# Attention's product with v turned round and scaled behind it, and an earlier bound for the seven-product form, in a two-layer trunk

## Chip, cores and metric

The kernel runs on one core of one Trainium2 chip. The metric is the device time of one execution in microseconds (us); the kernel before is given by the median of three runs.

## What is computed

One sequence of 1024 tokens of width 1024 passes two layers. Layer 0 mixes by sliding-window attention (8 query heads of 64, 2 key heads, window 128) and a gated delta rule (4 heads of 128); layer 1 by a recurrent block (RG-LRU). Each layer ends in a squared-relu MLP of width 4096, and a layer norm stands behind each mixer and each MLP. All of it is float32. The part that the change touches, cut from the reference:

```python
def sliding_window_attention(q, k, v, sinks):      # in blocks of W = 128 queries
    kb, vb = band(k), band(v)                      # the block before and this block
    s = jnp.einsum('bnqhgd,bnkhd->bnhgqk', qb, kb) * (DH ** -0.5)
    s = jnp.where(mask, s, -jnp.inf)
    p = jax.nn.softmax(jnp.concatenate([s, sink], axis=-1), axis=-1)[..., :-1]
    o = jnp.einsum('bnhgqk,bnkhd->bnqhgd', p, vb)

def sqrelu_mlp(x, w1, w2):
    h = jax.nn.relu(x @ w1)
    return (h * h) @ w2
...
for layer in range(DEPTH):                         # DEPTH = 2
    x = layer_norm(DN_ALPHA * x + mix, ...)
    x = layer_norm(DN_ALPHA * x + sqrelu_mlp(x, ...), ...)
```

## The kernel before

The 1024 tokens are two halves, c = 0 and c = 1, of 512 tokens (four blocks of 128). A large product goes in three passes of the faster type fp32r: each float32 operand is split into a high and a low part (a cast and a subtraction on ScalarE and VectorE), and `mm3` issues high x high, high x low, low x high into one PSUM bank. Such a pass over 128x512 is one record in the trace. A product of plain float32 operands is two records.

The order of TensorE's instructions is fixed when the kernel is built. A planner (`Clock`) keeps an estimated time for every engine; generators for the two halves (`stream`), and side streams (`mixers`: attention blocks, the middle part of the delta rule, layer norms), hand out their next matmul when the planner thinks its operands ready. TensorE, VectorE, ScalarE and SP (which issues most of the loads) run in the order written.

All calls on the other engines go through one helper, L178 in the profile; matmuls through L206, transposes by TensorE through L210. So rows are told apart by the names of tiles: `mm` and `mx` are PSUM banks, `ws` a loaded weight block, `wh`/`wl` its parts, `g` large tiles, `t`, `s`, `f` smaller ones, `vraw` the values of a block, `asc` the small numbers of an attention block, `csb` the constants with the identity matrix, `parked` tiles that wait in DRAM, `t_0_0_105` and its kind sums of weights in DRAM.

`attn_block` handles one block of 128 queries and all 8 heads. It multiplies queries and keys, masks, takes the exponentials (one ScalarE call for each head, with their sum), scales each head's probabilities by the reciprocal of that sum (again a ScalarE call each), transposes them on TensorE, copies the transposed tiles out of PSUM, and multiplies: v's 64 columns are the weights, 512 columns of probabilities move. The sum over the two key blocks gathers in one bank. The block gives 4 such products (2 in the very first block).

The second half's heads: `head_front` makes k, q and v of a delta-rule head by projection and convolution, `head_z` its gate z. For later heads the projections are made early and parked in DRAM (`park`: product, copy, store by SP) and loaded again (`f<-parked`). `head_mid` inverts a triangular matrix in four levels (`t<-t` matmuls of 32x32, between VectorE operations on `t`) and then runs the scan. When a half's mixer is done, `mix_out` loads the residual (`g<-x`, four loads of 512 KB on ScalarE's queue), makes the output projection (`out_proj`) and the layer norm.

`mlp` takes the hidden dimension in eight blocks (e = 0 to 7). `straight` does one block by plain products; `seven` does two by seven products in place of eight, with sums of weight quarters that `w2_sums` makes in DRAM (for each sum a 1 MB copy by SP, then a 1 MB load with accumulation by POOL; the two are issued 8 us or more apart by the planner's clock in layer 0). A half turns from `straight` to `seven` at an even block when there is room: half 1 at once, half 0 only when the other half has finished its projection (`sts[1]["op"]`). `first(j)` makes the eight hidden blocks that the first `seven` needs.

Of the kernel before, what the change touches and what calls it, by code (L numbers as in the profile page):

```python
# [12 lines left out]
AF = mybir.ActivationFunctionType  # L13
ALU = mybir.AluOpType
# [3 lines left out]
P = 128  # L18
# [6 lines left out]
GB = 14  # L25
# [188 lines left out]
def trunk(ctx: ExitStack, tc, I, out):  # L214
    nc = tc.nc
    clk = Clock(tc, nc)
    V, G, S, PE = clk.engine(nc.vector, "V"), clk.engine(nc.gpsimd, "G"), clk.engine(nc.scalar, "S"), clk
    DS, DA, DG = clk.engine(nc.sync, "V"), clk.engine(nc.scalar, "V"), clk.engine(nc.gpsimd, "V")
    at = lambda *a: lambda: clk.ready(*a)
# [12 lines left out]
    def nm(s):  # L232
        uid[0] += 1
        return f"{s}_{uid[0]}"

    rings = dict(RINGS, g=GB)
# [39 lines left out]
    def mx_ps():  # L276
        return clk.tile("mx", 4, pmx.tile([P, 512], F32, tag="mx", name=nm("mx")))

    def v4(a):
        return a.rearrange("p (a b) -> p a b", a=4)  # L280

    def bc_last(a, n):
        return a.unsqueeze(2).to_broadcast([P, a.shape[1], n])
# [9 lines left out]
    ident, U, M1 = C["ident"], C["U"], C["M1"]  # L293
# [100 lines left out]
    def split_ps(h, l, ps):  # L394
        S.copy(h, ps)
        V.tensor_tensor(l, ps, h, ALU.subtract)
# [134 lines left out]
    def mlp(layer, c, yT, yg, ls, res, tail=False):  # L531
# [185 lines left out]

        hids = {}
        e = 0
        while e < 8 and not ((c == 1 or sts[1].get("op", -1) >= layer) and rings["g"] >= 2 and e % 2 == 0):  # L720
            if e == 7:
                res["start"]()
            yield from straight(e, e == 7)
            e += 1
# [93 lines left out]
    def attn_block(c, n, st, oT, tl, o):  # L818
        vr = st["v"][n]
        yield from wait(lambda: "ok" in o)  # L820
        qT, kT = o["qT"], o["kT"]
        pk, pv = att["kT"], att["v"]
        keys = ([(pk, pv)] if pk is not None else []) + [(kT, vr)]
        att["kT"], att["v"] = kT, vr
        k0 = 2 - len(keys)
        w = len(keys) * P
        sc = cpool.tile([P, 40], F32, tag="asc", name=nm("asc"), bufs=2)
        mx, nmx, den, es = (sc[:, i * 8:(i + 1) * 8] for i in range(4))
        pm = []
        for gp in range(2):  # L830
            yield lambda: max(clk.ready(qT, kT), clk.bank("mx", 4, 2))
            ps = [mx_ps().rearrange("p (g k) -> p g k", g=2) for _ in range(2)]
            for g2 in range(2):
                g = 2 * gp + g2
                for i, (kk, _) in enumerate(keys):
                    for h in range(2):
                        PE.matmul(ps[h][:, g2, i * P:(i + 1) * P], qT[h * 64:(h + 1) * 64, g * P:(g + 1) * P],
                                  kk[h * 64:(h + 1) * 64, :], start=True, stop=True)
            for h in range(2):
                pt = tl[2 + 2 * gp + h].rearrange("p (g k) -> p g k", g=2)  # L840
                for g2 in range(2):
                    i = 2 * (2 * gp + g2) + h
                    V.tensor_tensor_reduce(pt[:, g2, :w], ps[h][:, g2, :w], C["amask"][:, k0 * P:], 1.0, NEG,
                                           ALU.add, ALU.max, mx[:, i:i + 1])
                pm.append(pt)
        V.scalar_tensor_tensor(nmx, mx, -0.125, nsink, ALU.mult, ALU.min)
        V.tensor_tensor(es, W["sinks"], nmx, ALU.add)
        for m in range(4):
            for g2 in range(2):
                i = 2 * (2 * (m // 2) + g2) + m % 2  # L850
                S.activation(pm[m][:, g2, :w], pm[m][:, g2, :w], AF.Exp, bias=nmx[:, i:i + 1], scale=0.125,
                             accum_out=den[:, i:i + 1])
        S.activation(es, es, AF.Exp)
        V.tensor_tensor(den, den, es, ALU.add)
        V.reciprocal(den, den)
        for m in (0, 2, 1, 3):
            for g2 in range(2):
                i = 2 * (2 * (m // 2) + g2) + m % 2
                S.activation(pm[m][:, g2, :w], pm[m][:, g2, :w], AF.Copy, scale=den[:, i:i + 1])
        yield at(*pm)  # L860
        po = mx_ps()
        pend = None
        for i, (_, vv) in enumerate(keys):
            for h in range(2):
                ps = mx_ps()
                for g in range(4):
                    PE.transpose(ps[:, g * P:(g + 1) * P], pm[2 * (g // 2) + h][:, g % 2, i * P:(i + 1) * P], ident)
                pT = tl[(6, 7, 2, 3)[2 * i + h]]
                (S.copy if h else V.tensor_copy)(pT, ps)
                yield at(pT)  # L870
                PE.matmul(po[h * 64:(h + 1) * 64, :], vv[:, h * 64:(h + 1) * 64], pT, start=(i == 0),
                          stop=(i == len(keys) - 1))
        h, l = oT.quad(0, n)
        split_ps(h, l, v4(po))
        yield lambda: 0.0


# [497 lines left out]
    sts = st  # L1375
# [32 lines left out]
    while streams or mixers:  # L1408
        m = next((m for m in mixers if m[0]() + MARGIN <= clk.now), None) if clk.bank("mx", 4) <= clk.now else None
# [144 lines left out]
```

## Time and profile before

| | |
|---|---|
| median of 3 runs | 2275.01 us (2270.06 to 2276.08) |
| profiled execution, its own time | 2275.25 us |
| its span | 2273.5 us |
| TensorE busy | 2212.7 us, 97% of the span |
| VectorE busy | 1546.0 us, 68% |
| ScalarE busy | 1048.4 us, 46% |
| chain that ended last | TensorE 85%, VectorE 7%, ScalarE 5%, DMA 2% |

A row of the timeline gives a start, a duration, the engine, the line, the operation, output<-inputs, the sizes and a count; a time in square brackets is idle time ahead of it, with the engine and tile that ended it. The records of pipelined matmuls overlap in a timeline (0.4 us for one, while the next starts 0.23 us later), so the cost of a matmul is read from the distance of two starts.

### The profile page before, as it was taken

The page shows a single profiled execution, that of the slowest core. Times are in us where ns is not written, and L with a number is a line of the kernel's source. Part 1 is how long each engine was busy: PE and PEld are TensorE (multiplying, and loading weights), DVE is VectorE, ACT ScalarE, POOL GpSimd, SP SyncE. Part 2 cuts the span into 40 slices and gives each one's busy share as a digit, 9 for nine tenths or more (in the row PEclk, how much of TensorE's full clock was granted, in tenths as well). Part 3 has the DMA queues.
Part 4 walks back from the last instruction along what each step waited for, and adds up shares of the span by engine and source line. Part 5 has one row for each costly group of instructions (what it writes and reads, how often), then busy time and mean ns, then how long its engine had stood idle before and what let it go on. Part 6 is the DMA issues. An engine that isn't in the chain of part 4 may idle for free.

```text
span 2273.5 us, 31954 instructions
## 1 busy us (share of the span) xinstructions
PE 2212.7 (97%) x12436; PEld 1788.5 (79%) x12436; DVE 1546.0 (68%) x2809; ACT 1048.4 (46%) x1878; POOL 28.6 (1%) x56
## 2 busy tenths in 40 slices
PE   8999999989999999999999999999999999999997
PEld 7776877758778887888887878878788887888886
DVE  6787676576555567596567898685566657776477
ACT  5365456244322344454444677373434444444442
POOL 0000000000000000000000000000000000000000
PEclk9999999989999999999999999999999999999999
DMA  4121223256667766677765333323533443444341
GB/s 162 57 77 49 94 79 112 84 181 181 188 199 221 210 209 201 205 251 224 237 214 184 126 134 115 127 83 98 179 103 123 140 145 128 150 169 146 122 164 67
DMA packets 89945, 337.46 MB, mean 148 GB/s; under 512 B 9921, under 2 KB 10305, under 8 KB 81601
## 3 DMA queue, kind: packets, MB, share of 16 engines
q1 hardware_dynamic: 76688, 280.56, 36.2%
q0 software_dynamic: 4608, 33.56, 7.8%
q10 hardware_dynamic: 8496, 21.30, 2.7%
q8 instruction: 97, 1.59, 0.3%
q14 instruction: 56, 0.45, 0.1%
HBM read 324.37 MB, written 78.12 MB: 177 GB/s over the span
## 4 chain that ended last, share of the span: by engine, by line
PE 85%; DVE 7%; ACT 5%; DMA 2%; issue 1%; ACTq 0%; SPq 0%; DVEq 0%
PE mm L206 67%; PE mx L206 17%; DVE g L178 2%; PE mx L210 2%; DVE wl L178 2%; ACT g L178 1%; DVE s L178 1%; ACT s L178 1%; ACT wh L178 1%; DVE t L178 1%; DVE f L178 1%; ACT t L178 1%; ACT f L178 1%; DMA f<-parked 1%; DMA parked<-r 0%
## 5 line engine op out<-in xcount | busy, mean ns | idle before, releaser
L206 PE MATMUL mm<-g,wh 128*128 128x512 f32 x2816 | 885.6, 396 | 1.1 <-DVE g L178 1.1
L178 DVE TENSOR_TENSOR wl<-ws,wh 128x1024 fp32r<-128x1024 f32 (+1 forms) x444 | 538.3, 1212 | 398.9 <-ACT wh L178 394.4
L178 ACT CAST wh<-ws 128x1024 fp32r<-128x1024 f32 (+1 forms) x356 | 371.3, 1043 | 663.4 <-PE mm L206 551.3
L206 PEld LDWEIGHTS mm<-g,wh 128*128 128x128 f32 x2816 | 521.5, 189 | 109.1 <-DVE g L178 2.8
L206 PE MATMUL mm<-g,wl 128*128 128x512 f32 x1408 | 550.3, 391 | 0.0
L206 PE MATMUL mm<-wh,s 128*128 128x512 f32 x1152 | 377.4, 394 | 0.7 <-DVE g L178 0.7
L206 PEld LDWEIGHTS mm<-g,wl 128*128 128x128 f32 x1408 | 265.4, 188 | 56.5
L206 PEld LDWEIGHTS mm<-wh,s 128*128 128x128 f32 x1152 | 216.9, 188 | 46.5 <-ACT s L178 1.1
L206 PE MATMUL mm<-wh,g 128*128 128x512 f32 (+1 forms) x768 | 240.0, 384 | 7.1 <-ACT wh L178 6.8
L206 PE MATMUL mm<-wl,s 128*128 128x512 f32 x576 | 224.8, 390 | 0.0
L206 PE MATMUL mx<-wh,s 128*128 128x512 f32 x576 | 187.9, 392 | 1.5 <-DVE s L178 1.5
L206 PEld LDWEIGHTS mm<-wh,g 128*128 128x128 f32 x768 | 143.3, 191 | 34.1 <-ACT wh L178 6.8
L178 ACT CAST s<-g 128x512 fp32r<-128x512 f32 x172 | 104.7, 622 | 103.2 <-PE mm L206 54.2
L178 DVE TENSOR_TENSOR s<-g,s 128x512 fp32r<-128x512 f32 x172 | 116.0, 685 | 44.3 <-ACT s L178 44.2
L206 PE MATMUL mm<-wl,g 128*128 128x512 f32 (+1 forms) x384 | 144.2, 375 | 0.2 <-DVE wl L178 0.2
L206 PEld LDWEIGHTS mx<-wh,s 128*128 128x128 f32 x576 | 108.2, 188 | 24.6 <-DVE s L178 2.4
L206 PEld LDWEIGHTS mm<-wl,s 128*128 128x128 f32 x576 | 108.6, 189 | 21.4 <-issue 0.2
L206 PE MATMUL mx<-wl,s 128*128 128x512 f32 x288 | 112.1, 389 | 0.0
L178 DVE CAST wh<-ws 128x1024 fp32r<-128x1024 f32 x88 | 60.4, 687 | 65.0 <-PE mm L206 57.7
L178 DVE TENSOR_TENSOR g<-g,mm 128x512 f32<-128x512 f32 x136 | 89.0, 682 | 11.9 <-PE mm L206 11.3
L178 ACT ACTIVATE g<-mm 128x512 f32<-128x512 f32 x100 | 59.2, 592 | 75.2 <-PE mm L206 75.2
L206 PEld LDWEIGHTS mm<-wl,g 128*128 128x128 f32 x384 | 73.5, 192 | 11.6 <-DVE wl L178 0.5
(234 smaller groups left out, 2390.7 us busy)
## 6 DMA issues: line engine op xcount, KB each, us to landing
ws<-w SPq DMA_DIRECT2D x232, 512.0 KB, 3.4
ws<-t SPq DMA_DIRECT2D x96, 512.0 KB, 3.4
t<-w POOLq DMA_DIRECT2D x32, 1024.0 KB, 9.1
ws<-hin_fm SPq DMA_DIRECT2D x32, 512.0 KB, 3.3
t<-w SPq DMA_DIRECT2D x16, 1024.0 KB, 6.8
t<-t SPq DMA_DIRECT2D x16, 1024.0 KB, 6.3
ws<-rin SPq DMA_DIRECT2D x32, 512.0 KB, 3.3
ws<-hout SPq DMA_DIRECT2D x16, 512.0 KB, 3.7
```

Source lines behind the costliest of these rows:

```text
L178: r = f(*a, **k)
L206: ins = self.pe.matmul(out, lhsT, rhs, start=start, stop=stop, skip_group_check=fresh)
L210: return self._pe(self.pe.transpose(out, x, ident), out, [x], 0.00042 * 2 * out.shape[-1])
```

## The change

Two places are edited. In `attn_block` the product is turned: the transposed probabilities of one head (128x128) are the weights and v's 64 columns move, 16 products a block (8 in the first). The probabilities are no longer scaled on ScalarE before it; the result, in which queries lie on partitions, is scaled by one VectorE operation with the broadcast reciprocals, and four transposes bring it back to the layout that the next step needs. The copies of the transposed probabilities are shared between ScalarE and VectorE by another rule. In `mlp`, half 0 of layer 0 may turn to `seven` when the second half has finished three heads' scans and four large tiles are free; half 0 with the other half's projection done, and half 1, go as before. In every other case it now asks for `GB` = 14 free large tiles, which is all there are.

```diff
@@ -717,7 +717,9 @@
 
         hids = {}
         e = 0
-        while e < 8 and not ((c == 1 or sts[1].get("op", -1) >= layer) and rings["g"] >= 2 and e % 2 == 0):
+        room = lambda: rings["g"] >= (2 if c == 1 or sts[1].get("op", -1) >= layer else
+                                      4 if layer == 0 and sts[1].get("scan", 0) >= 3 else GB)
+        while e < 8 and not (room() and e % 2 == 0):
             if e == 7:
                 res["start"]()
             yield from straight(e, e == 7)
@@ -853,25 +855,33 @@
         S.activation(es, es, AF.Exp)
         V.tensor_tensor(den, den, es, ALU.add)
         V.reciprocal(den, den)
-        for m in (0, 2, 1, 3):
-            for g2 in range(2):
-                i = 2 * (2 * (m // 2) + g2) + m % 2
-                S.activation(pm[m][:, g2, :w], pm[m][:, g2, :w], AF.Copy, scale=den[:, i:i + 1])
-        yield at(*pm)
-        po = mx_ps()
-        pend = None
-        for i, (_, vv) in enumerate(keys):
-            for h in range(2):
+        pT = {}
+        for h in range(2):
+            yield at(pm[h], pm[2 + h])
+            for i in range(len(keys)):
                 ps = mx_ps()
                 for g in range(4):
                     PE.transpose(ps[:, g * P:(g + 1) * P], pm[2 * (g // 2) + h][:, g % 2, i * P:(i + 1) * P], ident)
-                pT = tl[(6, 7, 2, 3)[2 * i + h]]
-                (S.copy if h else V.tensor_copy)(pT, ps)
-                yield at(pT)
-                PE.matmul(po[h * 64:(h + 1) * 64, :], vv[:, h * 64:(h + 1) * 64], pT, start=(i == 0),
-                          stop=(i == len(keys) - 1))
+                pT[i, h] = tl[(6, 7, 2, 4)[2 * h + i]]
+                (S.copy if i else V.tensor_copy)(pT[i, h], ps)
+                yield lambda: 0.0
+        yield at(*pT.values())
+        po = mx_ps()
+        for g in range(4):
+            for h in range(2):
+                o = po[:, (2 * g + h) * 64:(2 * g + h + 1) * 64]
+                for i, (_, vv) in enumerate(keys):
+                    PE.matmul(o, pT[i, h][:, g * P:(g + 1) * P], vv[:, h * 64:(h + 1) * 64], start=(i == 0),
+                              stop=(i == len(keys) - 1))
+        y = tl[3]
+        V.tensor_tensor(y.rearrange("p (i d) -> p i d", i=8), po.rearrange("p (i d) -> p i d", i=8), bc_last(den, 64),
+                        ALU.mult)
+        yield at(y)
+        ps = mx_ps()
+        for g in range(4):
+            PE.transpose(ps[:, g * P:(g + 1) * P], y[:, g * P:(g + 1) * P], ident)
         h, l = oT.quad(0, n)
-        split_ps(h, l, v4(po))
+        split_ps(h, l, v4(ps))
         yield lambda: 0.0
 
 
```

The order of instructions changes from the attention blocks on. On TensorE, a part of one attention block before (`mx_3795` is the bank that gathers the result, `g_146` and `g_147` hold probabilities, `t` is a delta-rule head at its level steps, `mm` a projection):

```order
L206 MATMUL mx_3795<-g_147,vraw_325 64x512
L210 MATMUL mx_3828<-csb,g_146 128x128 x2
L210 MATMUL mx_3828<-csb,g_147 128x128 x2
L206 MATMUL mm_3770<-g_2008,wh_3766 128x512
L206 MATMUL mm_3770<-g_2009,wh_3766 128x512
L206 MATMUL mm_3770<-g_2008,wl_3767 128x512
L206 MATMUL mx_3837<-t_3388 32x32 x16
L206 MATMUL mm_3770<-g_2008,wh_3766 128x512
L206 MATMUL mm_3770<-g_2009,wh_3766 128x512
L206 MATMUL mm_3770<-g_2008,wl_3767 128x512
L206 MATMUL mx_3795<-g_147,vraw_325 64x512
```

and after, the end of the products of a block (`t_1733` belongs to a delta-rule head):

```order
L206 MATMUL mx_2074<-vraw_315,g_146 128x64
L206 MATMUL mx_2074<-vraw_320,g_147 128x64
L206 MATMUL mx_2074<-vraw_315,g_147 128x64
L206 MATMUL mx_2074<-vraw_320,g_147 128x64
L206 MATMUL mx_2074<-vraw_315,g_146 128x64
L206 MATMUL mx_2074<-vraw_320,g_147 128x64
L210 MATMUL mx_2092<-csb,t_1733 128x128 x4
L206 MATMUL mm_1994<-g_234,wh_1990 128x512
L206 MATMUL mm_1994<-g_236,wh_1990 128x512
L206 MATMUL mm_1994<-g_234,wl_1991 128x512
```

The products of a block now stand in one piece behind all its transposes; the four transposes back (from `g_146`) follow a good twenty rows later, behind products of two projections.

At the end of the second half's heads, VectorE works in this order before (`t_4413` is the head at its level steps; `f_5070` and `f_5071` belong to a gate, the `f_56` tiles to convolutions of the last head, `wh` and `wl` to weights):

```order
L178 SCALAR_TENSOR_TENSOR f_5070<-f_5070,f_5071 128x512
L178 TENSOR_TENSOR t_4413<-t_4413,mx_5195 128x128
L178 STREAM_TRANSPOSE t_4413<-t_4413 128x128
L178 TENSOR_TENSOR g_4833<-f_5070,g_4832 128x512
L178 SCALAR_TENSOR_TENSOR f_5643<-f_5642,sm,f_5643 128x512 x3
L178 TENSOR_TENSOR t_4413<-mx_5224,csb 128x128
L178 SCALAR_TENSOR_TENSOR f_5654<-f_5653,sm,f_5654 128x512 x3
L178 TENSOR_TENSOR t_4413<-t_4413,mx_5251 128x128
L178 CAST wh_5420<-ws_5418 128x1024
L178 STREAM_TRANSPOSE t_4413<-t_4413 128x128
L178 SCALAR_TENSOR_TENSOR f_5665<-f_5664,sm,f_5665 128x512
```

and after (`t_4644` is the head, `f_5104` and `f_5248` belong to gates, `f_5105` and `f_5249` are their loads):

```order
L178 TENSOR_TENSOR t_4644<-mx_5167,csb 128x128
L178 SCALAR_TENSOR_TENSOR f_5104<-f_5104,f_5105 128x512
L178 TENSOR_TENSOR s_5113<-r_5152,s_5112 128x512
L178 TENSOR_TENSOR t_4644<-t_4644,mx_5194 128x128
L178 TENSOR_TENSOR g_4802<-f_5104,g_4801 128x512
L178 STREAM_TRANSPOSE t_4644<-t_4644 128x128
L178 TENSOR_TENSOR t_4644<-mx_5223,csb 128x128
L178 TENSOR_TENSOR wl_5431<-ws_5428,wh_5430 128x1024
L178 TENSOR_TENSOR t_4644<-t_4644,mx_5268 128x128
L178 STREAM_TRANSPOSE t_4644<-t_4644 128x128
L178 TENSOR_TENSOR t_4644<-mx_5296,csb 128x128
L178 SCALAR_TENSOR_TENSOR f_5248<-f_5248,f_5249 128x512
```

The steps on `t` now alternate with the multiplications of two gates, of which each needs a tile loaded from DRAM; before, one gate and the convolutions stand there. On ScalarE, the residual loads of the second half's output projection stood among the copies of a parked tile and of the layer norm (`r_5067` is a parked tile on its way, `g_4818` to `g_4832` are normed activations and mixer outputs):

```order
L178 CAST wh_5366<-ws_5364 128x1024
L178 COPY r_5067<-mm_5024 128x512
L178 DMA g_7293<-x 128x1024 x2
L178 DMA g_7294<-x 128x1024
L178 CAST g_4832<-f_4941 128x512
L178 ACTIVATE f_5001<-f_5002 128x512
L178 DMA g_7294<-x 128x1024
L178 CAST g_4820<-mx_5096 128x4x128
```

and now stand among weights of the MLP and of the projection (`g_7369` is a hidden block of `first`):

```order
L178 CAST wh_7448<-ws_7446 128x1024
L178 CAST wh_7478<-ws_7476 128x1024
L178 ACTIVATE g_7369<-mm_7377 128x512
L178 DMA g_7404<-x 128x1024 x2
L178 DMA g_7405<-x 128x1024
L178 ACTIVATE g_7369<-g_7369 128x512
L178 DMA g_7405<-x 128x1024
L178 CAST wh_7509<-ws_7507 128x1024
L178 CAST wh_7551<-ws_7549 128x1024
```

They moved behind the norm and behind the last head's scan. SP's order there is, before:

```order
L178 DMA parked_5066<-r_5067 128x512
L178 DMA ws_5522<-w_0 128x1024
L178 DMA f_5071<-parked_5066 128x512
L178 DMA f_5642<-parked_4089 128x512
L178 DMA t_0_0_105<-w_0 128x2048
L178 DMA f_5653<-parked_4148 128x512
L178 DMA f_5664<-parked_4286 128x512
L178 DMA ws_5579<-w_0 128x1024
L178 DMA ws_5721<-w_0 128x1024
L178 DMA t_0_0_106<-w_0 128x2048
```

and after:

```order
L178 DMA f_4999<-parked_4994 128x512
L178 DMA t_0_0_105<-w_0 128x2048
L178 DMA parked_5100<-r_5101 128x512
L178 DMA ws_5487<-w_0 128x1024
L178 DMA f_5105<-parked_5100 128x512
L178 DMA ws_5551<-w_0 128x1024
L178 DMA parked_5244<-r_5245 128x512
L178 DMA ws_5595<-w_0 128x1024
L178 DMA f_5249<-parked_5244 128x512
L178 DMA t_0_0_106<-w_0 128x2048
L178 DMA parked_5324<-r_5325 128x512
```

The stores and loads of three parked gates now stand between the copies of the first two sums (`t_0_0_105`, `t_0_0_106`), where before there were the loads of one gate and of the last head. The counts: TensorE has 30 products of 64x512 (v as weights, by the order's own way of naming) fewer, 120 of 128x64 and 32 transposes of 128x128 more; all products of 128x512 on split operands are as many as before; ScalarE has 64 scalings fewer, VectorE 8 operations of 128x512 more; the number of DMAs is the same. Half 0 of layer 0 turns to `seven` at its fifth block (e = 4) in both; in the changed order the first hidden block of `first` (24 products, `mm_7377`) stands ahead of the second half's output projection, and 96 products lie between the issue of the residual loads and the first row that uses one.

## Rows read from the trace of the kernel before

**Rows 1.** The page: the span, the busy time of the engines, and the granted clock in 40 slices of the span.

```profile
span 2273.5 us, 31954 instructions
...
PE 2212.7 (97%) x12436; PEld 1788.5 (79%) x12436; DVE 1546.0 (68%) x2809; ACT 1048.4 (46%) x1878; POOL 28.6 (1%) x56
...
PEclk9999999989999999999999999999999999999999
```

**Rows 2.** Windows of the zone of the last heads of the second half. Columns: the stretch and its length; busy time and number of instructions of TensorE, its weight loads, VectorE, ScalarE and POOL; granted clock; DMA share; GB/s.

```profile
461.00:472.00 11.00, 8.68 (x74) 6.84 (x73) 11.00 (x20) 8.72 (x14) 0.00 (x0) 1.00 0.40 138
472.00:481.00 9.00, 6.49 (x69) 4.58 (x73) 8.55 (x16) 4.34 (x8) 0.00 (x0) 0.62 0.99 385
490.00:498.00 8.00, 2.91 (x42) 1.98 (x41) 3.22 (x6) 2.45 (x4) 0.00 (x0) 0.98 0.50 117
498.00:508.00 10.00, 9.77 (x69) 6.99 (x70) 4.03 (x8) 3.05 (x5) 0.10 (x1) 0.50 0.32 105
```

**Rows 3.** Waits of TensorE in 440:525: what it waited for, us in total, times, longest.

```profile
PE mx L206 <- DVE t L178: 8.2, 5, 4.7
PE mx L210 <- DVE g L178: 3.1, 1, 3.1
```

**Rows 4.** Timeline of TensorE around one old product with v (first half). Columns: start, duration, engine, line, operation, output<-inputs, rows*columns of the array, size of the moving operand, count.

```profile
118.89 0.40 PE L206 MATMUL mm<-g,wl 128*128 128x512 f32 x1
119.21 1.07 PE L206 MATMUL mx<-g,vraw 128*64 128x512 f32 x2
120.22 0.66 PE L210 MATMUL mx<-csb,g 128*128 128x128 f32 x4
```

**Rows 5.** Groups of instructions by form: the old product with v (records; busy time, mean ns).

```profile
L206 PE MATMUL mx<-g,vraw 128*64 128x512 f32 x60 | 32.2, 618 | 0.0
```

**Rows 6.** Timeline of TensorE: the distance of records. Two starts with 36 products of the split form between them (first lines); 128x16 moving columns; four transposes and eight records of 128x128; 64x64.

```profile
22.35 0.62 PE L206 MATMUL mm<-g,wh 128*128 128x512 f32 x2
...
30.52 0.39 PE L206 MATMUL mm<-g,wh 128*128 128x512 f32 x1
...
32.56 0.51 PE L206 MATMUL mx<-dsc,csb 128*128 128x16 f32 x4
32.92 0.48 PE L206 MATMUL mm<-g,wh 128*128 128x512 f32 x1
...
448.78 0.60 PE L210 MATMUL mx<-csb,t 128*128 128x128 f32 x4
449.22 1.06 PE L206 MATMUL mx<-t 128*128 128x128 f32 x8
450.11 0.28 PE L206 MATMUL mx<-t,t 128*128 128x128 f32 x1
...
516.17 0.67 PE L206 MATMUL mx<-t,t 64*64 64x64 f32 x8
516.78 0.38 PE L206 MATMUL mx<-S,t 128*128 128x128 f32 x1
```

**Rows 7.** First half: a wait of TensorE and ScalarE's work ahead of it (the first row is from the chain of waits of 180:192, start, us, what; then ScalarE's timeline, TensorE's, and the form of the scalings and exponentials).

```profile
182.46 4.05 ACT g L178 x16
...
187.22 0.61 ACT L178 ACTIVATE s<-f 128x512 f32<-128x512 f32 x1
...
188.76 0.55 PE L210 MATMUL mx<-csb,s 128*128 128x128 f32 x3 [3.23 <-DVE s L178]
...
L178 ACT ACTIVATE g<-g,asc 128x256 f32<-128x256 f32 x112 | 50.7, 496 | 9.1 <-DVE asc L178 9.1
```

**Rows 8.** The zone of the last heads: three pieces of the chain of waits of 440:500 (start, us, what); then timeline rows of ScalarE (ACTq is its DMA issue) and of POOL.

```profile
470.67 7.59 DMA parked<-r
...
478.34 3.77 DMA f<-parked
...
487.25 7.31 DMA f<-parked
...
469.11 1.05 ACT L178 CAST wh<-ws 128x1024 fp32r<-128x1024 f32 x1
469.39 0.83 ACTq L178 DMA_DIRECT2D g<-x  x2
470.05 0.59 ACT L178 COPY r<-mm 128x512 f32<-128x512 f32 x1
...
482.19 0.63 ACT L178 ACTIVATE f<-f 128x512 f32<-128x512 f32 x1 [2.20 <-DMA f<-parked]
...
486.09 0.94 POOL L178 DMA_DIRECT2D t<-w  x1 [310.58 <-DMA t<-w]
```

**Rows 9.** DMA issues of 400:560: tiles, queue, count, KB each, median us from issue to landing.

```profile
g<-x ACTq DMA_DIRECT2D x4, 512.0 KB, 7.8
...
f<-parked SPq DMA_DIRECT2D x7, 256.0 KB, 3.3
parked<-r SPq DMA_DIRECT2D x4, 256.0 KB, 2.1
```

**Rows 10.** Timeline of TensorE (two waits at level steps) and of VectorE (a gate's multiplication).

```profile
476.82 0.65 PE L206 MATMUL mx<-t 32*32 32x32 f32 x32 [1.73 <-DVE t L178]
...
498.23 0.65 PE L206 MATMUL mx<-t 32*32 32x32 f32 x32 [4.69 <-DVE t L178]
...
482.86 0.69 DVE L178 SCALAR_TENSOR_TENSOR f<-f,f 128x512 f32<-128x512 f32 x1 [2.15 <-ACT f L178]
```

## Prediction

> **What bounds the kernel now.** The page comes first: TensorE is busy for 97% of the span, and its clock stands at nine tenths or more in all fortieths of the span but one, the ninth, from 455 to 512 us [rows 1]. Its instructions run in the order in which the planner wrote them, so the time can fall only if its own work gets shorter or one of its waits goes. The profiled execution took 2275.25 us, 0.24 above the median of the three timed runs, so the sum below is made against 2275.25 and needs no correction. That slice is also where the diff moves work, the end of the second half's heads, so I split it into windows [rows 2]. Four things are to be seen. In 461:472 VectorE is busy for 11.00 of 11.00 us and TensorE for 8.68. In 472:481 the DMA share is 0.99 and the granted clock 0.62. In 490:498 TensorE works for 2.91 of 8.00 us. In 498:508 the clock is 0.50, that is, the lower of its two levels (1.2 GHz) all through, right after a stretch in which TensorE had little work. The waits of TensorE in the zone [rows 3] are 8.2 us for VectorE's `t` (level steps of a head) and 3.1 us for VectorE's `g` (the layer norm). What the two edits can give is therefore small: a per mille of the time for the product with v, and some of those waits.
>
> **The product with v.** It goes by records: each of the 30 old products is two records of 128x512, and takes 120.22 - 119.21 = 1.01 us; the record ahead of it lasts 119.21 - 118.89 = 0.32 us in place of the 0.227 of its kind [rows 4, 6], so entering the narrow form costs 0.09. The 30 cost 30 x 1.10 = 33.0 us of TensorE, all on the path, since TensorE hardly idles; there are 60 records in the trace [rows 5]. In their place stand 120 products of 128x64, two records each, so 240, and 32 more transposes. A record of 128x128 with new weights each time takes (450.11 - 449.22) / 8 = 0.111 us; one with 16 moving columns (32.92 - 32.56) / 4 = 0.090, so an eighth of the columns saves a fifth; the shortest kind, 64x64, (516.78 - 516.17) / 8 = 0.076; a transpose (449.22 - 448.78) / 4 = 0.110 [rows 6]. 64 columns lie between 16 and 128, so I take 0.100: 240 x 0.100 + 32 x 0.110 = 27.5 us. That **saves 5.5 us**. (A product of 128x512 in the split form takes (30.52 - 22.35) / 36 = 0.227, three of them to a step [rows 6]; this is used below.) The bounds are 0.111 (30.1, saves 2.9) and 0.076 (21.8, saves 11.2).
>
> **The scaling behind the product.** 64 scalings on ScalarE go, 56 of them 128x256 (half of the 112 rows of that form; the others are exponentials, which stay) [rows 7], and 8 VectorE products over 128x512 come. ScalarE is busy for less than half of the span [rows 1], so nearly all of this lies beside other work. One place doesn't: in the first half TensorE waits 3.23 us before 188.76 for the tile `s` of a head, whose tanh at 187.22 stood on ScalarE behind eight exponentials, 4.05 us from 182.46 [rows 7]. The scalings themselves come after it. But with another length of each block the planner places them elsewhere, and in the changed order no tanh of such a tile stands behind exponentials, though the start of a convolution still does. I take **2 us** off, since something else may be late there; the ends are 0 and 3.2. The new VectorE operation of 0.7 us (as others over 128x512, 0.69 [rows 10]) is waited for by four transposes of a block, but these are run as a side stream that TensorE reaches late, with other products ahead; nothing is charged for it, and at most 8 x 0.7 = 5.6 if none of it is hidden.
>
> **What the `room` edit moves.** It allows `seven` where the second half has finished three of its heads. The order shows that the switch comes at the same block (the fifth, e=4) in both kernels, so as many products of 128x512 are issued as before: the edit **does not give what its words say**, fewer products. What it does is to let the first of the eight hidden blocks of `first`, the work ahead of the first seven, go before the second half's output projection (24 products). With it the four residual loads on ScalarE's queue, 512 KB each, move: before, they are issued from 469.39 on [rows 8], and fill the DMA rows of 472:481. There the store of a parked tile takes 7.59 us where its fellows take a median of 2.1 [rows 8, 9], and SP's queue, all following loads with it, waits behind it: the next load of a parked tile starts at 478.34. In the changed order they stand beside the products of the second half's projection, with 96 products, 21.8 us, ahead of the first use; such a load takes 7.8 us [rows 9], so that is cover enough. If it weren't, the price would be the rest of one load, below 8.
>
> In the layer-norm stretch the order now has five parked projections (120 products, 27 us at 0.227) between the projection and the end of the norm, in place of four and level steps that need VectorE. Before, TensorE waits there 3.1 [rows 3] and 1.73 [rows 10], and the 0.62 of clock over 9.00 us means 6.8 us at half speed, with TensorE busy for 6.49 of 9.00: 6.8 x 0.72 / 2 = 2.4 lost. I leave 1 us of wait and no half clock: **-3.8 and -2.4**. Ends: nothing, and the whole 7.2.
>
> Behind the norm the level steps of the last head now stand between the loads of gates z1, z2 and z3, where before they stood between two gates and the convolutions. VectorE runs in order, so a gate's multiplication that waits for its load holds the level step behind it, and TensorE with it. That is the **new wait**. Before, the stretch cost 8.2 - 1.73 = 6.4 us of waits, its longest 4.69 at 498.23 [rows 10], and some 5 us by the half clock (10 us at 0.50, TensorE busy for 9.77 [rows 2]). After, by hand for z1: cast 1.05, copy 0.59, store 2.1, load 7.3 (the length of the one beside POOL's accumulation issued at 486.09; 3.3 otherwise), tanh 0.63, multiplication 0.69, and some 2.2 of smaller steps and hops (transpose, split, a step over 128x128): 14.6 [rows 8 to 10]. TensorE has 45 products and two steps meanwhile, 45 x 0.227 + 2 x 0.5 = 11.2 (a step's 32 records end within 0.65 of their start [rows 10]), so it waits 3.4. For z2 the load is the 3.3 one and a cast of 0.7 stands ahead: 11.3 against 36 products and three steps, 9.5: 1.8. For z3 the copy of the second sum is queued ahead of it, so 14.6 again, against 30 products, three steps and z2's wait, 10.0: 4.6 (0.6 with a short load). Together 9.8, which is 3.4 more than before; the half clock stays as it was. **+3.4**, from -2 (all loads 3.3) to +26 (rival 2).
>
> Sum: -5.5 - 2 - 3.8 - 2.4 + 3.4 = -10.3, and 2275.25 - 10.3 = **2265.0**. A measurement of this kernel can tell about 0.3%, 6.8 us, from no change.
>
> **A rule against it.** A record with 16 columns costs four fifths of one with 128 [rows 6], so in both what counts is loading the weights, not the columns. The Trainium skill, TensorEngine Tiling (Array Packing), section When to Use Tiling, advises for a right side of 64 columns or fewer the swap of stationary and streaming operand; before is that swapped form, and the change undoes it. What that would make of the time here is the third rival.
>
> **The rivals.** (1) *The waits only change places*: the layer norm keeps its stalls because VectorE remains full there [rows 2], and the level steps take 3.4 more. Then -5.5 - 2 + 3.4 = -4.1, **2271**. For it speaks that VectorE had no free microsecond in 461:472; against it that the level steps, the work which needs it, leave that stretch.
>
> (2) *Slower: each of the three gate loads lies beside a 1 MB copy of the sums and is waited for in full.* Each then exposes 7.4 us, and each wait brings a stretch of half clock like that of 498:508, 5 us: 3 x 12.4 = 37.2 in place of 11.4, +25.8. With the other terms, -13.7, the time is **2287**. It decides from about 25 us of loss in that stretch. For it: a load beside the accumulation took 7.31 where the median is 3.3 [rows 8, 9]. Against: the sums come every 8 us or more, one after another, and the walk above finds only two of three beside one.
>
> (3) *The turned product loads its weights in the open.* If loading (0.090) and the columns (an eighth of the 0.505 of an old record, 0.063) add up, a record takes 0.153, and 240 x 0.153 + 3.5 = 40.2, which is 12.7 more than taken: **2278**. Against it: with 128 columns the two together took 0.111 [rows 6], so they overlap.
>
> (4) *The columns decide*: 240 x 0.063 + 3.5 = 18.6, 8.9 less than taken: **2256**. Against it the 16-column row.
>
> **How the numbers follow.** Forecast 0.45, its own range 2257 to 2272 from the terms' ends. Rival 1: 0.25. Rival 2: 0.15. Rival 3: 0.07. Rival 4: 0.08. The bound for faster is 2268.2: of the forecast 0.32 lies below it, of rival 1 0.06, of rival 4 all 0.08, so 0.46. Slower needs 2282: 0.14 of rival 2 and 0.03 of rival 3, so 0.17. The rest, 0.37, is within 0.3%. The range 2254 to 2280 leaves out most of rival 2 and a little below.
>
> **What would show it.** The turned product: 16 records of 128x64 (eight of a block's 16 products) that take 16 x 0.100 = 1.6 us from the first to the next instruction, 1.8 or 1.2 at the bounds, 2.45 by rival 3. The scaling: the wait of 3.23 before 188.76 at about 1. The layer norm: no wait above 1 us there and a clock of 1.00, with the parked stores at 2 us; a stretch at 0.5 or waits of 5 in sum would be rival 1. The level steps: three waits of about 3.4, 1.8 and 4.6 for VectorE's `t`, each with a load of a parked tile behind it; above 20 us in sum is rival 2. The residual loads: no wait of the projection's accumulation for them. The forecast falls if later stretches, where the two orders agree, change by more than 2 us, since nothing above speaks of them.

## The result, and the profile after

The changed kernel takes 2276.93 us (median of 20 runs, 2270.09 to 2280.89) against 2269.74 for the kernel before in the runs beside it: **1.0029 times as long (95% interval 1.0021 to 1.0038)**, slower by some 6.6 us. The forecast was 2265, with 2254 to 2280 as its range; measured from 2275.25 it said 0.45% faster. The profiled execution took 2280.89 us, 5.6 more than the one before, so the two traces show a difference of about the size to be explained. Both traces are of long executions: 2275.25 lies 5.5 above the median of the 20 runs of before, 2280.89 lies 4.0 above that of the changed kernel.

The page after, to be held against [rows 1]:

```profile
span 2279.1 us, 32326 instructions
...
PE 2211.1 (97%) x12648; PEld 1815.2 (80%) x12648; DVE 1550.8 (68%) x2818; ACT 1022.4 (45%) x1813; POOL 28.5 (1%) x56
...
PEclk9999999989999999999999999999999999999999
```

TensorE is busy for 1.6 us less, in a span that is 5.6 us longer: it stands idle for 7.2 us more. The windows of the zone of the last heads, as in [rows 2]:

```profile
461.00:472.00 11.00, 10.74 (x107) 8.29 (x106) 8.06 (x15) 5.82 (x10) 0.94 (x1) 1.00 0.62 140
472.00:481.00 9.00, 1.68 (x22) 1.08 (x23) 2.41 (x5) 2.29 (x4) 0.00 (x0) 0.80 0.47 158
...
490.00:498.00 8.00, 7.56 (x123) 5.58 (x122) 3.74 (x7) 1.58 (x3) 0.82 (x1) 1.00 0.76 251
498.00:508.00 10.00, 2.37 (x24) 1.75 (x22) 2.26 (x5) 2.96 (x6) 0.00 (x0) 0.84 0.56 118
```

The layer norm's stretch is mended: VectorE is no longer full in 461:472 (8.06 us), and TensorE works for 10.74 of 11.00 us. But in 472:481 and 498:508 TensorE works for 1.68 and 2.37. The waits of TensorE in 440:525, for [rows 3]:

```profile
PE mx L206 <- DVE t L178: 15.6, 4, 7.6
```

The wait for VectorE's `g` is gone; that for `t`, the level steps, went from 8.2 to 15.6 us. Where it comes from is read from the chain of waits of 440:515 (start, us, what), with the issues of POOL (timeline) and VectorE's row below it:

```profile
465.00 2.35 DMA parked<-r
...
467.37 9.81 DMA f<-parked
...
490.98 3.03 DMA parked<-r
...
494.07 10.89 DMA f<-parked
...
464.91 0.94 POOL L178 DMA_DIRECT2D t<-w  x1 [286.38 <-DMA t<-w]
493.66 0.82 POOL L178 DMA_DIRECT2D t<-w  x1 [27.81 <-DMA t<-w]
...
505.71 0.69 DVE L178 SCALAR_TENSOR_TENSOR f<-f,f 128x512 f32<-128x512 f32 x1 [10.79 <-ACT f L178]
```

Two gates' loads of 256 KB take 9.81 and 10.89 us, issued 2.5 and 0.4 us behind an accumulation of 1 MB on POOL's queue; in the second case VectorE stands 10.79 us in front of the gate's multiplication, with a level step behind it, and TensorE waits. The load between the two, beside no accumulation, took 3.6.

To see where the 5.6 us went, I added up, over each stretch of both traces, by how much the distance of two starts of TensorE exceeds the usual one of that form (stalls and half clock together; the sums are worked out from all rows of a trace, and depend on what is taken as usual by some 0.4 us). The first row also has what the product itself saves, 2.6:

| stretch | forecast | traces |
|---|---|---|
| heads, to 450 us | -7.5 (product -5.5, scaling -2) | +1.6 |
| zone of the last heads, 450 to 525 | -2.8 (norm -6.2, level steps +3.4) | +0.6 |
| the rest | 0 | +3.4 |
| sum | -10.3 | +5.6 |

Of the 15.9 us between forecast and traces, 9.1 lie in the heads, 3.4 in the zone and 3.4 behind it. The zone of the last heads is, by this count, hardly worse than before; it loses its time by other waits.

### The profile page after: what moved, and what is told of

Read it like the earlier page. It is cut to its first block, busy times and chain, and to the rows that moved or that the text cites. A ratio compares the mean times of both kernels' runs of the same rounds, so it can differ in the third digit from the quotient of the medians.

```text
span 2279.1 us, 32326 instructions
## 1 busy us (share of the span) xinstructions
PE 2211.1 (97%) x12648; PEld 1815.2 (80%) x12648; DVE 1550.8 (68%) x2818; ACT 1022.4 (45%) x1813; POOL 28.5 (1%) x56
## 4 chain that ended last, share of the span: by engine, by line
PE 86%; DVE 6%; ACT 3%; DMA 2%; issue 1%; ACTq 0%; SPq 0%; DVEq 0%
PE mm L206 68%; PE mx L206 17%; DVE g L178 2%; PE mx L210 2%; DVE wl L178 1%; DMA f<-parked 1%; DVE s L178 1%; ACT s L178 1%; ACT wh L178 1%; ACT t L178 1%; DVE t L178 0%; ACT f L178 0%; DMA ws<-w 0%; ACT g L178 0%; DMA parked<-r 0%
## 5 line engine op out<-in xcount | busy, mean ns | idle before, releaser
L206 PEld LDWEIGHTS mm<-wl,g 128*128 128x128 f32 x384 | 73.5, 192 | 11.2 <-issue 0.5
```

Source lines behind the costliest of these rows:

```text
L206: ins = self.pe.matmul(out, lhsT, rhs, start=start, stop=stop, skip_group_check=fresh)
```

## The experiments

All ratios are to the kernel before on the same chip, with 95% intervals; "moved alone" below means the third run.

**Which edit, and are the sums to blame?** Four kernels; the edits are

```diff
 pv_only            # the turned product with the old condition for seven
 room_only          # the old product with the new condition
 after_sums_later, before_sums_later
-            spawn(w2_sums())
+            spawn(w2_sums(), clk.now + 60.0)
```

> Only the attention product is turned and scaled behind; the condition for seven products is that of before. Theory 1 (the turned product saves little, and its other lengths move the last head's level steps between the loads of the parked gates, which are slow beside the sums' accumulations): the order of that zone is the changed kernel's, so two waits of 7 us or more for VectorE's t appear there again, and the time is that of the changed kernel, ratio to before 1.001 to 1.004. Theory 2 (the other edit, with the first hidden block and the residual loads in another place, is what costs): ratio 0.998 to 1.000, because the turned product then gives its 2 to 5 us.

> Only the condition for seven products is changed; the attention product is that of before. Theory 1: the zone of the last heads keeps the order and the waits of before (4.7 us the longest for VectorE's t), and the ratio to before is 0.999 to 1.001. Theory 2: ratio 1.002 to 1.004.

> The changed kernel, with the sums of weight quarters in DRAM started 60 us later by the planner's clock, so that no copy or accumulation of them lies beside the loads of the parked gates. Theory 1: these loads land in 3 to 4 us in place of 9.8 and 10.9, the two waits of 7.3 and 7.6 us for VectorE's t fall to 3 us together or less, and the time falls by 8 to 14 us against the changed kernel: ratio to before 0.996 to 0.999. Theory 2: the waits may fall, but the time stays within 0.1% of the changed kernel, since what costs lies elsewhere (1.002 to 1.004).

> The kernel before, with the sums started 60 us later as in the run beside it. Theory 1: the load of 7.31 us lands in 3 to 4 and the wait of 4.69 us behind it falls below 1.5, with less of the half clock behind it: ratio 0.997 to 0.999. If loads beside sums are not what the waits are made of: the wait of 4.69 stays, ratio 0.999 to 1.001.

Measured: pv_only **1.0046 (1.0033 to 1.0059)**, just above Theory 1's range, room_only **1.0004 (0.9991 to 1.0017)**, after_sums_later **0.9958 (0.9946 to 0.9971)**, before_sums_later **1.0002 (0.9989 to 1.0015)**. The second edit does nothing by itself: in its trace TensorE, VectorE and ScalarE run the forms and tile families of before, in the same order. The turned product costs time, and brings the zone's order with it (TensorE's is that of the changed kernel up to 781 us, VectorE's up to 490). But the loss of pv_only is made up of other parts. Its waits for `t` in 440:530 are 9.0 us in two, less than Theory 1 wanted; its order holds 24 products of 128x512 more, 5.4 us, since without the second edit half 0 is late for one `seven`; and TensorE waits 6.31 us for `g` before 1481.53 (in before 1.1 us in all at that place). So the second edit does give something, one `seven` that the turned product alone would lose; the count against the kernel before did not show that.

With the sums moved, 16 us come back (1.0029 to 0.9958, just more than Theory 1 asked) and the changed kernel beats both. TensorE's order stays the same to the end, and VectorE's and ScalarE's up to 509 us, so in the zone only the transfers differ. TensorE's waits in 440:525 are then

```profile
PE mx L206 <- DVE t L178: 0.6, 1, 0.6
```

The stretch 950:1050 is mended too: TensorE is busy there for 100.00 us, against 97.83 in the changed kernel. So the move takes away more than the change had added, losses that the zone of before has as well. What the turned block costs in the heads stays (waits of 10.0 us in 125:450).

The same move gives the kernel before nothing. Its waits for `t` fell as expected (8.2 to 2.1 us), but its time did not. Its wait for the layer norm, 2.9 us, stays, and so does half clock (0.56 in 472:481, 0.68 in 481:490). In 950:1050 its trace has a new slow load of weights, issued 0.2 us behind an accumulation (chain of waits of 960:985), and 2 us lost behind it:

```profile
965.30 9.95 DMA ws<-w
```

Whether that is all that took the place of the waits in the timed runs is open.

**Is it the order of VectorE, the sums' kind or the queue?** Edits to the changed kernel:

```diff
 after_gate_later, after_gate_30           # 12.0 and 30.0
             DS.dma_start(ps, parked[b])
+            t = clk.now + 12.0
+            yield lambda: t
 after_both_later                          # 12.0 and the sums 60 us later
 after_sums_100                            # the sums 100 us later
 after_plain_pool
-                yield behind(8.0 + 4.0 * layer, DG, layer, j, k, 1, accum_op=ALU.add)
+                yield behind(8.0 + 4.0 * layer, DG, layer, j, k, 1)
 after_gate_actq
-            DS.dma_start(ps, parked[b])
+            DA.dma_start(ps, parked[b])
```

> The changed kernel with its sums where they are, but with 12 us of the planner's time between the load of a parked gate and its first use, so that fewer level steps stand behind a gate's multiplication on VectorE. Theory 1 (the loss is VectorE's order: level steps behind a gate whose load is slow): the loads still take 8 to 11 us, the waits for VectorE's t in this zone fall from 15.5 us to 6 or less, ratio to before 0.997 to 1.000. Theory 3 (the accumulations slow whatever is loaded there, weights too): the waits turn up at other loads, ratio 1.002 to 1.004.

> The changed kernel with its sums where they are and 30 us of the planner's time between the load of a parked gate and its first use, since with 12 us the gates' multiplications still stood ahead of the level steps. Theory 1 (the loss is level steps behind a gate whose load is slow): loads of 8 to 11 us remain, but no wait above 2 us for VectorE's t in the zone, ratio to before 0.996 to 0.999. Theory 3 (the accumulations slow whatever is loaded there): waits of 5 us or more stay in the zone behind other loads, ratio 1.001 to 1.004.

> The changed kernel with both: sums 60 us later and gates used 12 us after their load. Theory 1: with fast loads there is nothing left to gain from the second, the time is that of the sums moved alone, ratio to before 0.995 to 0.997. If other waits for gates are left: below 0.995.

> The changed kernel with the sums 100 us later in place of 60. Theory 1 (what counts is that they no longer lie beside the gates' loads): as with 60, ratio to before 0.995 to 0.997. If 60 hit a lucky phase of the sums against the loads of the MLP: 0.998 or more.

Measured: after_gate_later **1.0026 (1.0011 to 1.0041)**, after_gate_30 **1.0049 (1.0035 to 1.0064)**, after_both_later **0.9948 (0.9932 to 0.9963)**, after_sums_100 **0.9964 (0.9949 to 0.9979)**. The first two missed the range of Theory 1. With 12 us, a gate's multiplication still stood ahead of the level steps, behind loads of 9.99 and 9.52 us. With 30 us it did not, but the loads of the last head's convolutions came in its place (chain of waits of 480:520, and VectorE's row):

```profile
490.01 8.17 DMA f<-parked
...
498.95 0.75 DVE L178 SCALAR_TENSOR_TENSOR f<-f,sm,f 128x512 f32<-128x512 f32 x1 [10.80 <-ACT f L178]
```

TensorE waited 18.2 us for `t` there. So Theory 1 in its narrow form, that the gates alone are the matter, falls; what was called Theory 3 fits: other loads beside a sum are late as well, and the in-order engines hold the level steps behind them. (Not each of them: of the three convolution loads issued together at 489.58, behind an accumulation of 489.16, the first took 2.8 us.) Moving the sums is what helps, by 60 or 100 us, and waiting 12 us with the gates adds nothing to it within the noise. The two moves don't differ by more than the noise either; the trace of the second has a wait of 4.7 us before 979.80, behind a chain with a weight load of 8.00 us from 959.19 on, beside work of a layer norm.

> The changed kernel, in which POOL's second transfer of each sum is a plain copy of 1 MB in place of an accumulation; the sums are therefore not sums, and the MLP computes something else at equal cost. TensorE's, VectorE's and SP's orders are those of the changed kernel. If it is the accumulation that holds the engines: the gates' loads land in 3 to 6 us, the two waits of 7 us fall below 3 each, ratio to before 0.995 to 0.999. If it is any 1 MB on POOL's queue: loads of 8 to 11 us and a ratio of 1.001 to 1.004.

> The changed kernel, with the loads of the parked gates issued by ScalarE in place of SP; the sums are where they are. If the 16 DMA engines are what is shared: loads of 8 to 11 us beside the accumulations and a ratio of 1.001 to 1.005 (more, if ScalarE's queue stands still behind a wait for the store). If SP's queue is what delays them: loads of 3 to 5 us, ratio 0.996 to 0.999.

Measured: after_plain_pool **0.9991 (0.9982 to 1.0000)**, after_gate_actq **1.0032 (1.0019 to 1.0045)**. The plain copy takes about half of the loss away, and ends just above the first expectation; its chain has

```profile
459.26 5.51 DMA parked<-r
...
464.79 2.60 DMA f<-parked
...
485.35 9.61 DMA f<-parked
```

Over the whole trace the plain copy of 1 MB lands in a median of 5.4 us where the accumulation takes 8.9. The first copy, issued at 458.42, held the store (5.51 us), and the first gate's load came after it. The second, issued 0.4 us ahead of a load, made that load as slow as an accumulation does. So a plain 1 MB delays a load too; accumulating lasts longer.

In after_gate_actq the time is that of the changed kernel, but no gate's load lies behind an accumulation, so what its expectation asks, loads beside the accumulations, was not put to the test. The chain and SP's timeline have

```profile
454.07 8.23 DMA f<-parked
...
484.34 6.87 DMA f<-parked
...
453.00 0.61 SPq L178 DMA_DIRECT2D t<-w  x1
...
483.45 0.51 SPq L178 DMA_DIRECT2D t<-w  x1
```

Two of the gates' loads, now on ScalarE's queue, were issued 1.1 and 0.9 us behind 1 MB copies on SP's queue and took 8.23 and 6.87 us; the two others took 2.7. TensorE's waits for `t` were 7.5 us in place of 15.6; why the timed runs gained nothing from that is open. Since a load behind a transfer on another queue is late as well, the order within SP's queue is not the cause. The Trainium skill, DMA: Bandwidth & Descriptors, section Issuing engines are not separate DMA queues, says that all issuing engines end in the same 16 DMA engines; the loads of 8.23 and 6.87 us agree.

**What does the product cost?** Each product is issued a second time right behind the first, and TensorE's other work keeps its order:

```diff
 turned_twice, old_twice       # sums 60 us later; the old one adds again
+    def again(self, out, lhsT, rhs, start, stop):
+        ins = self.pe.matmul(out, lhsT, rhs, start=start, stop=stop)
+        self.tc.add_manual_dep(ins.ins, self.last.ins.name, NOSYNC, reason="order")
+        self.last = ins
```

> The changed kernel with its sums 60 us later (median 2257.9 us), and each of the 120 turned products issued a second time right behind the first, without the planner counting it, so that the order of everything else stays; the result is the same. At 0.112 us a record, as the trace of the changed kernel has it, the time rises by 240 x 0.112 = 26.9 us; at the forecast's 0.100 by 24.0; if the weights are loaded in the open, by 37. Ratio to before 1.0065 to 1.0085 at 0.112.

> The kernel before with its sums 60 us later (median 2269.2 us), and each of the 30 old products issued a second time right behind the first, added once more, so that attention's part of the output is doubled; the order of everything else stays. If an old product costs 1.01 us and entering the form 0.09 once, the time rises by 30 x 1.01 = 30.3 us, ratio to before 1.0125 to 1.0145. The difference to the run beside it is the saving of the turned form, 3.4 us, ahead of its 32 transposes.

Measured: turned_twice **1.0080 (1.0068 to 1.0092)**, 1.22% above the sums moved alone, 27.7 us; old_twice **1.0120 (1.0107 to 1.0134)**, 1.18% above its base, 26.8 us. By the intervals each of the two sums is good to some 4 us, so the traces decide. The first is 0.115 a record. The trace of the changed kernel has 0.110 in one block (32 records of 128x64, and what follows: 186.93 - 183.41 = 3.52 us) and 0.112 as the median distance of all 240.

```profile
183.41 3.68 PE L206 MATMUL mx<-vraw,g 128*128 128x64 f32 x32
186.93 0.61 PE L210 MATMUL mx<-csb,t 128*128 128x128 f32 x4
```

The second is 3.5 less than expected, within that noise, but the timeline of old_twice shows a reason (L210 is the repeat):

```profile
118.78 1.07 PE L206 MATMUL mx<-g,vraw 128*64 128x512 f32 x2
119.69 1.02 PE L210 MATMUL mx<-g,vraw 128*64 128x512 f32 x2
120.65 0.66 PE L215 MATMUL mx<-csb,g 128*128 128x128 f32 x4
```

A second product behind one of its own kind adds 1.87 - 1.01 = 0.86 us, not 1.01: part of the 1.01 is entering and leaving the narrow form. So an old product costs 1.10 with both, and 30 of them 33.0 as forecast, but the turned ones cost 240 x 0.112 = 26.9 with 3.5 for transposes, and the saving is 2.6. (It may be a us more: the four transposes behind an old product take 120.71 - 120.22 = 0.49 us in the trace of before, and four elsewhere 0.44.)

**What are the scalings worth?** Three kernels:

```diff
 front_scaled_sums_later      # sums 60 us later; planned
+        for m in (0, 2, 1, 3): ... S.activation(pm[m][:, g2, :w], ..., AF.Copy, scale=den[:, i:i + 1])
-        V.tensor_tensor(y..., po..., bc_last(den, 64), ALU.mult)
+        V.tensor_copy(y, po)
 extra_scalings               # sums 60 us later; not counted by the planner
+                nc.scalar.activation(pm[m][:, g2, :w], pm[m][:, g2, :w], AF.Copy, scale=1.0)
 before_unscaled              # counted, not issued
-                S.activation(pm[m][:, g2, :w], pm[m][:, g2, :w], AF.Copy, scale=den[:, i:i + 1])
+                clk.issue("S", [x], [x, z], clk.NS["S"][0] + 0.093 + clk.NS["S"][1] * w)
```

> The changed kernel with sums 60 us later, but the probabilities are scaled on ScalarE ahead of the turned product, as before, and VectorE only copies the product out. If taking 64 scalings off ScalarE is worth time (the forecast's 2 us): slower than the run with the sums moved alone (0.9958) by 2 us or more, ratio to before 0.997 to 0.999. If they lay beside other work: within 1.5 us of it, 0.9950 to 0.9965.

> The changed kernel with its sums 60 us later, and 64 scalings by 1 on ScalarE at the place where the kernel before scales the probabilities, without the planner counting them, so that the order of everything else stays; the result is the same. If the scalings lie beside other work, the time rises by less than 1.5 us, ratio to before 0.995 to 0.9965. By the forecast's term, 2 us, up to 3.2: 0.9965 to 0.9975. If the 20 us of the run with the scalings in front of the turned product come from the scalings themselves and not from the other order: above 1.000.

> The kernel before, with the 64 scalings counted by the planner but not issued, so that TensorE's order stays; attention's probabilities stay unscaled, so its output is another. By the forecast's term: 2 us faster, 0 to 3.2, ratio to before 0.9985 to 1.000. If the scalings are worth what putting them back cost (21 us): ratio 0.990 to 0.993.

Measured: front_scaled_sums_later **1.0045 (1.0030 to 1.0061)**, extra_scalings **1.0048 (1.0033 to 1.0064)**, before_unscaled **0.9990 (0.9979 to 1.0001)**. In the kernel before, taking the scalings out is worth 2.3 us, the forecast's term, though the interval goes from nothing to 4.8. Behind the turned product, putting them back costs 20 us either way, against 0.9958. In extra_scalings TensorE waits for them two or three times in each block but the first (waits of TensorE in 125:450; L860 are the scalings):

```profile
PE mx L210 <- ACT g L860: 13.6, 16, 1.8
```

The turned form has all transposes of a block next to each other and close behind the exponentials, so of 25.1 us of scalings on ScalarE 13.6 are waited for. In front_scaled_sums_later the planner knew of them, and the waits stood elsewhere (in 125:525 4.7 for ScalarE's `t`, 5.6 for VectorE's). Its 20 us are therefore the scalings and another order in one; that they would be the scalings alone isn't shown.

## Why the prediction was wrong

The sign was wrong, and it was missed in four steps: the size of the new wait, the product's record, the waits of the turned block, and what lies behind the zone.

*"+3.4, from -2 to +26": the new wait at the level steps.* The mechanism was right and named, its size was not. The waits rose by 9.1 us (from 6.4 to 15.6), not 3.4. The walk gave a load beside an accumulation 7.3 us, from one row [rows 8]; it took 9.81 and 10.89. The wait for z1 was 7.3 in place of 3.4, for z3 7.6 in place of 4.6, for z2 0.4 in place of 1.8. Put into the same walk, the measured loads give 14.6 + 2.5 - 11.2 = 5.9 for z1 and 14.6 + 3.6 - 10.0 = 8.2 for z3, so the load is the term that was mis-sized. Rival 2 had this mechanism and its sign; two of its three loads were exposed in full, though with less half clock than it charged. (In the walk, 36 products and three steps are 9.7 us, not 9.5; that changes nothing.)

*"-3.8 and -2.4": the layer norm.* Right: no wait for `g` is left there, the clock of 461:472 is 1.00 with TensorE busy, and the parked store took 2.35 us in place of 7.59. Half clock stands behind the two new waits instead (0.80 in 472:481, 0.84 in 498:508, before 0.62 and 0.50). Together with the level steps, the zone came out at +0.6 instead of -2.8.

*"That saves 5.5 us": the product with v.* 0.112 us a record, just above the upper bound, not 0.100; the saving is 2.6 by the traces. A record of 64 columns costs what one of 128 does [rows 6]. The fault was the 0.090 for 16 columns, and with it the interpolation by columns: that group of four stands between records of another form, and by its single records the first start lies 0.026 us ahead of the second, the others 0.112 apart. The other such group of before (timeline) takes (273.60 - 273.13) / 4 = 0.117:

```profile
273.13 0.62 PE L206 MATMUL mx<-dsc,csb 128*128 128x16 f32 x4 [0.33 <-DVE dsc L178]
273.60 0.48 PE L206 MATMUL mm<-wh,g 128*128 128x512 f32 x1
```

So from 16 to 128 columns, with new weights each time, the columns make no difference here. Rivals 3 (0.153) and 4 (0.063) fall. By the Trainium skill, TensorE: Matmul & The Clock Gate, section LDWEIGHTS (loading the stationary operand), 128 columns of weights take 128/1.2 = 107 ns; the 0.112 us agree within 5%. The rule of the swap, by which the old form is the better one, is not borne out: back to back the two forms cost the same within the noise (26.8 and 27.7 us above), and between other work the turned one is cheaper by 2.6 us, its transposes included.

*"2 us off": the scaling.* The size fits the kernel before (2.3, nothing to 4.8), and the wait of 3.23 [rows 7] is gone. But the forecast kept the rest of the heads as it was, and charged nothing for the turned block's own waits: TensorE's waits in 125:450 are 10.2 us in sum, before 8.3, among them

```profile
PE mx L210 <- DVE t L178: 2.4, 2, 1.4
PE mx L206 <- ACT t L178: 2.4, 1, 2.4
PE mx L210 <- DVE asc L178: 2.1, 3, 1.3
```

and some 3.4 us more were lost at half clock, in two stretches, near 133 and 177 us, that the trace of before doesn't have. Two terms of -7.5 thus became +1.6; not every part of that is traced to a row.

*"later stretches, where the two orders agree".* They cost 3.4 us more, nearly all in 950:1050, beside work of a layer norm (chain of waits of 984:1000):

```profile
979.02 9.57 DMA ws<-w
```

The sums had shifted against the loads of weights: an accumulation was issued at 978.00, 1.0 us ahead of this one, whose fellows take a median of 3.4. With the sums moved the loss is gone. The prediction treated orders that agree on TensorE as alike on the DMA queues too.

The forecast of 10 us less holds for the changed kernel with its sums out of the way (0.42%, 9.5 us, below before). That the size fits is luck: in that run the heads keep their loss, and the zone gains more than was forecast (waits of 0.6 us in 440:525).

## What to carry to other kernels

Before you move steps beside other transfers, look at what else loads there: here most 256 KB loads issued just behind a 1 MB transfer, on POOL's or on another queue, took 7 to 11 us in place of 3, and an engine that runs in order made TensorE wait for them. Test a suspected contention by moving the bulk transfer away before you mend the waits one by one; two repairs of single waits failed here, and moving the sums gave 16 us. When a planner sets the order, a local edit can change waits far from it by as much as it saves: here a sum of a few microseconds over ten rows of one execution did not give the sign.

## What the runs showed of the hardware that was not expected

A load issued just behind a bulk transfer lands about when that does. In the changed kernel loads of 9.81 and 10.89 us landed 2.4 us behind and 0.7 us ahead of accumulations that took 9.90 and 12.00; in after_plain_pool one of 9.61 landed 0.2 behind a copy that took 9.80; in after_gate_actq, from another queue, one of 8.23 landed 0.2 behind a copy that took 9.13. Loads beside none take some 3. One load of after_gate_30 that was issued 0.4 behind an accumulation took 2.8.

The narrow form of a plain float32 product (64 columns of weights, 512 moving) costs 0.86 us behind one of its kind, and 1.10 between others: 0.24 for entering and leaving. Plain float32 records with 128 columns of new weights are 0.112 us apart with 16, 64 or 128 columns moving.

The spread of the runs goes with the granted clock: the changed kernel takes 2270 to 2281 us at a mean clock of 0.990 to 0.995 (20 runs), with its sums moved 2255 to 2261 at 0.995 and 0.996 (5 runs). Of before, the runs beside pv_only go from 2264.91 at 0.996 to 2278.32 at 0.991. The trace that the prediction used (0.993) is one of the longer ones, so the half clock that it priced need not be that of a usual run.
